# Orders of TensorE and VectorE in the attention of a hybrid decoder layer: left to the scheduler, or written out in the kernel

## The chip, the core and the metric

The kernel runs on one core of a Trainium2 chip. A core has TensorE (PE in the rows; its weight loads are PEld), VectorE (DVE), ScalarE (ACT), GpSimd (POOL), and SyncE (SP), which here only issues DMAs. Each engine takes its instructions in one fixed order and waits at each until what it needs is there. The metric is the device time of one execution in microseconds (us).

## The reference

One decoder layer on 512 tokens of width 1024: RMS norm, one wide input projection, three token mixers (native sparse attention, a gated spatial MLP, an RWKV-7 recurrence), a merge of the three, an output projection, a gated per-layer embedding, a last norm.

```python
def _nsa(q, kc, vc, ks, vs, kw, vw, gate, ...):        # 8 heads of 64, 2 key groups
    ...
    def block(qb):                                     # 128 queries at a time
        p_c = _masked_softmax(q . k_cmp, valid_c)      # 31 compressed keys
        ...
        p_s = _masked_softmax(q . k_sel, valid_s)      # selected blocks: here all 8 of 8
        p_w = _masked_softmax(q . k_win, valid_w)      # window of 512: here all
        return gblk[..., 0:1] * o_c + gblk[..., 1:2] * o_s + gblk[..., 2:3] * o_w

zs = jnp.einsum('bsnc,ncd->bsnd', ys, w_branch[i])     # ys: the three mixers' outputs
merge = jax.nn.sigmoid(mg).reshape(B, S, N_BRANCHES, D)
x = x + jnp.sum(merge * zs, axis=2) @ w_o[i]
```

With 512 tokens the selection takes every block and the window covers every key, so both are plain causal attention with keys of their own.

## The kernel before

Every large product is made of three TensorE matmuls: each float32 operand is split into a high part and a rest (`wh` and `wl` for weights, `hH`/`hL`, `ysH`/`ysL`, `ph`/`pl` for data), and high x high, high x rest, rest x high add up in PSUM. ScalarE makes the high part (a cast), VectorE or GpSimd the rest (a subtraction).

**Attention.** Four query blocks `i` of 128 rows, the last first (`ATT` = 3, 2, 1, 0); block `i` sees `W` = (i+1)*128 keys. In each, two key groups `g`, and in each group two branches `b` (selected, window): 16 steps (i, g, b) with four heads each. A step is made of these parts:
- S0 to S3, the scores of a head: two matmuls of `W` columns and a mask matmul `trib` of 128 columns into `s_ps` (3 buffers); VectorE takes the row maximum `mx`, ScalarE the exponential into `P` with the row sum `sm`.
- norm: VectorE makes 1/`sm` times the branch's gate, and the four heads of `P` are scaled by it. `PS` names the engine for each head: "VVSG" is VectorE, VectorE, ScalarE, GpSimd.
- T0 to Ti, one per 128 keys: four transposes of `P` into `p_ps`; ScalarE casts to `ph`, VectorE subtracts for `pl`.
- O0 to Oi: two matmuls of 512 columns, `pl` then `ph`, into `o_ps` (one buffer). The last one of a group is followed by ScalarE's copy `ot` and two VectorE additions into `nsaY`.

Compressed keys: `sc_c` once per block and a small softmax on VectorE (`pcm`); per group a transpose `pc_ps`, VectorE's `pd`, ScalarE's `ph`, VectorE's `pl`, and the first two products into `o_ps` (`vcst`). `p_ps`, `pc_ps` and `sc_c` share two PSUM buffers (tag "pt").

**Merge.** For each branch b and each of 8 output chunks m, `merge` makes a gate product (24 matmuls of 512 columns from `hH`, `hL`; `sg` is its tanh) and a branch product (12 from `ysH`, `ysL`), multiplies on VectorE and adds on GpSimd into `macc`. Of branch 1, six gates were made earlier and are only loaded. Branches 1 and 2 need nothing from the attention; branch 0 needs all of it. Weights come by DMA into `wr` (4 buffers), ScalarE casts `wh`, GpSimd subtracts `wl` (5 buffers each).

**What sets the order.** The program is handed to a scheduler that runs its own timeline and places every instruction on its engine where it expects it to be ready. `HOLD` holds four chunks of branch 2 behind certain groups of the attention; the rest of the merge of branches 1 and 2 is filled in wherever the scheduler sees TensorE free.

Of the kernel before, what the change touches and what calls it, by code (L numbers as in the profile page):

```python
# [9 lines left out]
F32 = mybir.dt.float32  # L10
# [18 lines left out]
PS = "VVSG"  # L29
ATT = (3, 2, 1, 0)  # L30
HOLD = (-1,) * 12 + (3, 4, 5, 6)
# [14 lines left out]
def hybrid_kernel(ctx, tc, x, p, norm_g, w_in, cmp_w1, cmp_w2, cmp_pe, sg_ln_g, sg_ln_b, sg_w, sg_b,  # L46
# [742 lines left out]
    def merge(b, yH, yL, first, fin, after=()):  # L789
        for m in range(8):  # L790
          with ExitStack() as es:
            if m < len(after) and after[m] is not None:
                es.enter_context(tc.issue_after(after[m]))
            sg = gp.tile([128, 512], F32, tag="sg", name="sg")
            if b == 1 and m < NG:
                SY.dma_start(sg, dr["sg"][m * 128:(m + 1) * 128, :])
            else:
                fm_block(O_MG + b * 1024 + m * 128, 128, lambda ps: S.activation(sg, ps, AF.Tanh, scale=0.5))

            def ev_b(ps):  # L800
                if first:
                    V.scalar_tensor_tensor(macc[:, m, :], sg, 1.0, ps, op0=OP.add, op1=OP.mult)
                else:
                    V.scalar_tensor_tensor(sg, sg, 1.0, ps, op0=OP.add, op1=OP.mult)
                    (V if b == 0 and m == 7 else G).tensor_tensor(macc[:, m, :], macc[:, m, :], sg, OP.add)
                fin(m)
            fm_block(m * 128, 128, ev_b, w_branch[b], yH, yL, 4)
# [5 lines left out]
    anch = []  # L813
    for i in ATT:
        isl = slice(i * 128, (i + 1) * 128)
        W = (i + 1) * 128
        sc = aps.tile([128, 8, 64], F32, tag="pt", name="sc_c", bufs=BP)
        for h in range(8):
            mm(sc[:, h, :], qst[:, h // 2, h % 2, isl], kcst[:, h // 4].rearrange("p a n -> p (a n)"), True, True)
# [10 lines left out]
        gv = gate[:, i, :].rearrange("p (h b) -> p b h", b=3)  # L830
        if i == 0:
            V.scalar_tensor_tensor(sm8, sm8, rowm, gv[:, 0, :], op0=OP.mult, op1=OP.mult)
        else:
            V.tensor_tensor(sm8, sm8, gv[:, 0, :], OP.mult)
        V.tensor_tensor(pcm, pcm, sm8.unsqueeze(2).to_broadcast([128, 8, 32]), OP.mult)
        for g in range(2):
            o_ps = aps.tile([128, 512], F32, tag="o", name="o_ps", bufs=BO)
            pc_ps = aps.tile([128, 128], F32, tag="pt", name="pc_ps", bufs=BP)
            PE.transpose(pc_ps, pcm[:, 4 * g:4 * g + 4, :].rearrange("p h n -> p (h n)"), ident)
            pd = ap_.tile([128, 4, 128], F32, tag="pd", name="pd", bufs=1)  # L840
            ph = ap_.tile([128, 512], R, tag="ph", name="ph", bufs=3)
            pl = ap_.tile([128, 512], R, tag="pl", name="pl", bufs=3)
            V.tensor_tensor(pd, pc_ps.unsqueeze(1).to_broadcast([128, 4, 128]),
                            hm.unsqueeze(2).to_broadcast([128, 4, 128]), OP.mult)
            pd2 = pd.rearrange("p h t -> p (h t)")
            S.copy(ph, pd2)
            V.tensor_tensor(pl, pd2, f(ph), OP.subtract)
            mm(o_ps, vcst[:, g, :], ph, True, False)
            mm(o_ps[0:64], vcst[:, g, 0:64], pl, False, False)
            for b in range(2):  # L850
                P = ap_.tile([128, 4, 512], F32, tag="P", name="P")
                mx = ap_.tile([128, 4], F32, tag="mx", name="mx")
                sm = ap_.tile([128, 4], F32, tag="sm", name="sm")
                for hh in range(4):
                    h = g * 4 + hh
                    s_ps = aps.tile([128, 512], F32, tag="s", name="s_ps", bufs=BS)
                    qs = qst[:, h // 2, h % 2, isl]
                    mm(s_ps[:, :W], qs, kst[b][:, g, 0, :W], True, False)
                    mm(s_ps[:, :W], qs, kst[b][:, g, 1, :W], False, False)
                    mm(s_ps[:, i * 128:W], identb, trib, False, True)  # L860
                    V.tensor_reduce(mx[:, hh:hh + 1], s_ps[:, :W], axis=AX.X, op=OP.max, negate=True)  # L861
                    S.activation(P[:, hh, :W], s_ps[:, :W], AF.Exp, bias=mx[:, hh:hh + 1],  # L862
                                 accum_out=sm[:, hh:hh + 1])
                V.reciprocal(sm, sm)
                V.tensor_tensor(sm, sm, gv[:, 1 + b, g * 4:g * 4 + 4], OP.mult)
                for hh in range(4):
                    if PS[hh] == "S":
                        S.activation(P[:, hh, :W], P[:, hh, :W], AF.Copy, scale=sm[:, hh:hh + 1])
                    else:
                        (G if PS[hh] == "G" else V).tensor_scalar(P[:, hh, :W], P[:, hh, :W], sm[:, hh:hh + 1],  # L870
                                                                  None, op0=OP.mult)
                for kt in range(i + 1):
                    p_ps = aps.tile([128, 512], F32, tag="pt", name="p_ps", bufs=BP)
                    for hh in range(4):
                        PE.transpose(p_ps[:, hh * 128:hh * 128 + 128], P[:, hh, kt * 128:kt * 128 + 128], ident)  # L875
                    ph = ap_.tile([128, 512], R, tag="ph", name="ph", bufs=3)
                    pl = ap_.tile([128, 512], R, tag="pl", name="pl", bufs=3)
                    S.copy(ph, p_ps)  # L878
                    V.tensor_tensor(pl, p_ps, f(ph), OP.subtract)  # L879
                    mm(o_ps[0:64], vst[:, kt, b, g, 0:64], pl, False, False)  # L880
                    last = mm(o_ps, vst[:, kt, b, g, :], ph, False, b == 1 and kt == i)
            anch.append(last)
# [140 lines left out]
```

## Time and profile before

| | |
|---|---|
| runs | 747.08 us median of 3 (744.39 to 748.1) |
| profiled execution | 744.63 us, span 742.8 us |
| TensorE busy in the span | 714.5 us |
| VectorE, ScalarE, GpSimd busy | 408.6, 353.8, 287.0 us |
| first score of the attention, last product into `o_ps` | 378.1 and 562.4 us |
| granted TensorE clock, mean | 0.993 |

The span is the stretch that the profile covers; 1.8 us of the profiled execution lie around it. Positions below are microseconds from the span's start. Matmuls are pipelined: a record of 0.4 us does not mean that the next one starts 0.4 us later, so "busy" overstates how full TensorE is.

### The profile page before, as it was taken

The page shows a single profiled execution, that of the slowest core. Times are in us where ns is not written, and L with a number is a line of the kernel's source. Part 1 is how long each engine was busy: PE and PEld are TensorE (multiplying, and loading weights), DVE is VectorE, ACT ScalarE, POOL GpSimd, SP SyncE. Part 2 cuts the span into 40 slices and gives each one's busy share as a digit, 9 for nine tenths or more (in the row PEclk, how much of TensorE's full clock was granted, in tenths as well). Part 3 has the DMA queues.
Part 4 walks back from the last instruction along what each step waited for, and adds up shares of the span by engine and source line. Part 5 has one row for each costly group of instructions (what it writes and reads, how often), then busy time and mean ns, then how long its engine had stood idle before and what let it go on. Part 6 is the DMA issues. An engine that isn't in the chain of part 4 may idle for free.

```text
span 742.8 us, 13074 instructions
## 1 busy us (share of the span) xinstructions
PE 714.5 (96%) x4941; PEld 606.7 (82%) x4941; DVE 408.6 (55%) x776; ACT 353.8 (48%) x743; POOL 287.0 (39%) x275
## 2 busy tenths in 40 slices
PE   4999999999999999989999999989999999999995
PEld 4888788999878987779877778867877888998995
DVE  6531587758843863565676565397555223226345
ACT  6554555542363342335565554576554333227453
POOL 6444640120220263300144345333445565356563
PEclk9999999999999999999999999999999999999999
DMA  5853122125536364427433212201228334132212
GB/s 194 188 140 100 48 81 71 41 85 146 156 105 224 101 184 117 116 86 232 124 97 103 58 43 71 71 16 42 53 62 268 96 91 127 59 114 72 80 63 114
DMA packets 106689, 78.73 MB, mean 106 GB/s; under 512 B 5569, under 2 KB 97282, under 8 KB 106626
## 3 DMA queue, kind: packets, MB, share of 16 engines
q1 hardware_dynamic: 105890, 75.27, 35.5%
q10 hardware_dynamic: 736, 2.63, 0.9%
q8 instruction: 39, 0.64, 0.4%
q14 instruction: 24, 0.20, 0.1%
HBM read 67.91 MB, written 9.96 MB: 105 GB/s over the span
## 4 chain that ended last, share of the span: by engine, by line
PE 88%; DVE 4%; ACT 2%; DMA 2%; issue 1%; POOL 1%; SPq 1%; ACTq 0%; POOLq 0%; DVEq 0%
PE mm_ps L62 70%; PE s_ps L62 3%; PE o_ps L62 2%; PE g_ps L62 2%; PE p_ps L875 2%; DMA w1t<-in_cmp_w_dram 1%; PE Yp L62 1%; DVE mx L861 1%; PE u_ps L62 1%; ACT wh L78 1%; PE xt_ps L222 1%; PE r_ps L62 1%; PE mx_ps L62 1%; DVE pl L879 1%; PE bk_ps L477 1%
## 5 line engine op out<-in xcount | busy, mean ns | idle before, releaser
L79 POOL TENSOR_TENSOR wl<-wr,wh 128x512 fp32r<-128x512 f32 x144 | 192.6, 1346 | 278.9 <-ACT wh L78 257.6
L78 ACT CAST wh<-wr 128x512 fp32r<-128x512 f32 (+1 forms) x194 | 119.4, 620 | 166.5 <-PE mm_ps L62 114.9
L62 PE MATMUL mm_ps<-hH,wh 128*128 128x512 f32 (+1 forms) x440 | 174.9, 398 | 3.3 <-ACT wh L78 1.9
L62 PE MATMUL mm_ps<-hL,wh 128*128 128x512 f32 (+1 forms) x440 | 171.6, 390 | 0.0
L62 PE MATMUL mm_ps<-hH,wl 128*128 128x512 f32 (+1 forms) x440 | 171.1, 389 | 0.0
L62 PEld LDWEIGHTS mm_ps<-hH,wh 128*128 128x128 f32 x440 | 83.5, 190 | 20.7 <-ACT wh L78 2.2
L62 PEld LDWEIGHTS mm_ps<-hH,wl 128*128 128x128 f32 x440 | 83.2, 189 | 17.4 <-issue 0.2
L62 PEld LDWEIGHTS mm_ps<-hL,wh 128*128 128x128 f32 x440 | 83.6, 190 | 16.5 <-issue 0.2
L62 PE MATMUL mm_ps<-wh,hL 128*128 128x256 f32 (+1 forms) x224 | 65.0, 291 | 0.0
L62 PE MATMUL mm_ps<-wh,hH 128*128 128x256 f32 (+1 forms) x224 | 63.8, 286 | 0.0
L62 PE MATMUL mm_ps<-wl,hH 128*128 128x256 f32 (+1 forms) x224 | 63.7, 285 | 0.0
L79 DVE TENSOR_TENSOR wl<-wr,wh 128x512 fp32r<-128x512 f32 (+1 forms) x50 | 38.0, 768 | 26.8 <-ACT wh L78 26.7
L62 PEld LDWEIGHTS mm_ps<-wh,hL 128*128 128x128 f32 x224 | 42.2, 188 | 1.1 <-issue 0.5
L62 PEld LDWEIGHTS mm_ps<-wh,hH 128*128 128x128 f32 x224 | 42.1, 188 | 1.2 <-issue 0.5
L62 PEld LDWEIGHTS mm_ps<-wl,hH 128*128 128x128 f32 x224 | 42.2, 188 | 0.5
L879 DVE TENSOR_TENSOR pl<-p_ps,ph 128x512 fp32r<-128x512 f32 x40 | 27.1, 685 | 25.7 <-ACT ph L878 25.6
L62 PE MATMUL mm_ps<-ysH,wh 128*128 128x512 f32 x96 | 38.6, 402 | 0.1
L62 PE MATMUL mm_ps<-ysL,wh 128*128 128x512 f32 x96 | 38.4, 400 | 0.2 <-DVE ysL L725 0.2
L62 PE MATMUL mm_ps<-ysH,wl 128*128 128x512 f32 x96 | 38.2, 398 | 0.0
L862 ACT ACTIVATE P<-s_ps,mx 128x512 f32<-128x512 f32 (+3 forms) x64 | 33.4, 531 | 7.9 <-DVE mx L861 5.5
L62 PE MATMUL mm_ps<-wh,mH 128*128 128x256 f32 x128 | 35.9, 286 | 0.0
L62 PE MATMUL mm_ps<-wl,hT 128*128 128x256 f32 x128 | 35.8, 281 | 0.0
(337 smaller groups left out, 1434.6 us busy)
## 6 DMA issues: line engine op xcount, KB each, us to landing
wr<-in_w_in_dram SPq DMA_DIRECT2D x130, 256.0 KB
wr<-in_w_branch_dram SPq DMA_DIRECT2D x24, 256.0 KB
wr<-in_w_o_dram SPq DMA_DIRECT2D x16, 256.0 KB
wr<-in_w_ple_gate_dram SPq DMA_DIRECT2D x16, 256.0 KB
xs__129<-in_x_dram SPq DMA_DIRECT2D x4, 512.0 KB
w1t<-in_cmp_w_dram SPq DMA_DIRECT2D x4, 512.0 KB
x<-in_x_dram ACTq DMA_DIRECT2D x4, 512.0 KB
out_dram<-x SPq DMA_DIRECT2D x8, 256.0 KB
```

Of the source, the lines that this page charges most:

```text
L62: return PE.matmul(o, a, b, start=start, stop=stop, **kw).ins
L78: S.copy(h[:, :m], raw[:, :m])
L79: ph_["l"].tensor_tensor(l[:, :m], raw[:, :m], f(h[:, :m]), OP.subtract)
L222: PE.transpose(ps[:, k, :], xs_[:, t, (4 * a + k) * 128:(4 * a + k + 1) * 128], ident)
L477: PE.transpose(ps[:, c - c0, :], bk[:, c, 0:2].rearrange("p s t -> p (s t)"), ident)
L861: V.tensor_reduce(mx[:, hh:hh + 1], s_ps[:, :W], axis=AX.X, op=OP.max, negate=True)
L862: S.activation(P[:, hh, :W], s_ps[:, :W], AF.Exp, bias=mx[:, hh:hh + 1], accum_out=sm[:, hh:hh + 1])
L875: PE.transpose(p_ps[:, hh * 128:hh * 128 + 128], P[:, hh, kt * 128:kt * 128 + 128], ident)
L879: V.tensor_tensor(pl, p_ps, f(ph), OP.subtract)
```

## The change

The attention and the merge of branches 1 and 2 are written in one interleaved order. TensorE's matmuls and most VectorE instructions there go through `keep_in_program_order` (`pin`), which keeps them in the order in which the code calls them; ScalarE, GpSimd and the DMA queues are still placed by the scheduler.

- `merge_gen` yields before each merge matmul; `deal(n)` issues the next n. There are 432 of them (6 chunks of 12, 10 of 36). `FILL` = (4, 8, 6, 24): 38 around the scores of the first step, then 24 in each of the 16 steps, spread over the step's parts; the last 10 after the attention.
- `ORD` gives the order of the parts within a step. The S parts belong to the next step, L is the previous step's last O, C the two `vcst` products of a group's first step, P the `pc_ps` transpose of the next group in a group's second step. `cmp_` (`sc_c` and its softmax) of the next block comes behind S1 of the step (g, b) = (1, 0).
- `later(n, fn)` runs `fn` at the n-th `tick`; there is a tick behind each part. So `pl` and `nsaY` follow their own part directly on VectorE, and norm and the second half of `cmp_` follow one part later.
- `PS` is "VVSS": ScalarE scales the fourth head, where GpSimd did.
- `HOLD` is gone. `y0`'s four loads of `nz` land in `y0L` itself in place of a `gp` buffer; the merge of branch 0 is as before.

```diff
-PS = "VVSG"
+PS = "VVSS"
 ATT = (3, 2, 1, 0)
-HOLD = (-1,) * 12 + (3, 4, 5, 6)
+FILL = (4, 8, 6, 24)
...
+    def blk_gen(ws, srcH, srcL, nk, evac, ahead):
+        hs, ls = ws
+        ahead()
+        ps = pmm.tile([128, 512], F32, tag="mm", name="mm_ps")
+        for k in range(nk):
+            for j, (w, s) in enumerate(((hs, srcH), (hs, srcL), (ls, srcH))):
+                yield
+                pin(PE.matmul(ps, w[k], s[:, k, :], start=k == 0 and j == 0, stop=k == nk - 1 and j == 2))
+        evac(ps)
...
+    def later(n, fn):
+        late.append([n, fn])
+
+    def tick():
+        for e in list(late):
+            e[0] -= 1
+            if e[0] <= 0:
+                late.remove(e)
+                e[1]()
...
+    def s_(i, g, b, hh):
...
+        mmp(s_ps[:, i * 128:W], identb, trib, False, True)
+        pin(V.tensor_reduce(mx[:, hh:hh + 1], s_ps[:, :W], axis=AX.X, op=OP.max, negate=True))
+        S.activation(P[:, hh, :W], s_ps[:, :W], AF.Exp, bias=mx[:, hh:hh + 1], accum_out=sm[:, hh:hh + 1])
+
+        def norm():
+            pin(V.reciprocal(sm, sm))
+            pin(V.tensor_tensor(sm, sm, gvs[i][:, 1 + b, g * 4:g * 4 + 4], OP.mult))
+            for j in range(4):
+                if PS[j] == "S":
+                    S.activation(P[:, j, :W], P[:, j, :W], AF.Copy, scale=sm[:, j:j + 1])
+                else:
+                    pin(V.tensor_scalar(P[:, j, :W], P[:, j, :W], sm[:, j:j + 1], None, op0=OP.mult))
+        if hh == 3:
+            later(2, norm)
+
+    def t_(i, g, b, kt):
...
+        S.copy(ph, p_ps)
+        later(1, lambda: pin(V.tensor_tensor(pl, p_ps, f(ph), OP.subtract)))
...
+    ORD = {3: "S0 L T0 S1 T1 C S2 O0 S3 T2 O1 T3 P O2", 2: "S0 L T0 S1 T1 C S2 O0 S3 T2 P O1",
+           1: "S0 L T0 S1 C S2 O0 S3 P T1", 0: "S0 L T0 S1 C S2 P S3"}
+    fill = merge_gen(((1, y1H, y1L, True), (2, y2H, y2L, False)))
...
+        for j, act in enumerate(acts):
+            act()
+            tick()
+            deal((j + 1) * FILL[3] // len(acts) - j * FILL[3] // len(acts))
```

TensorE at group (i, g) = (0, 0), up to its two `vcst` products (part C) and the O part behind them. Before:

```order
L62 MATMUL s_ps<-kst_3738,qst 128x128 x2
L62 LDWEIGHTS identb
L62 MATMUL s_ps<-trib,identb 128x128
L62 MATMUL o_ps<-ph,vcst 128x512
L62 MATMUL o_ps<-pl,vcst 64x512
L62 MATMUL o_ps<-pl,vst 64x512
L62 MATMUL o_ps<-ph,vst 128x512
L839 MATMUL pc_ps<-ident,pcm 128x128
```

and in the changed kernel:

```order
L871 MATMUL s_ps<-kst_3738,qst 128x128 x2
L871 LDWEIGHTS identb
L871 MATMUL s_ps<-trib,identb 128x128
L799 MATMUL mm_ps<-hH,wl 128x512
L799 MATMUL mm_ps<-hH,wh 128x512
L799 MATMUL mm_ps<-hL,wh 128x512
L871 MATMUL o_ps<-ph,vcst 128x512
L871 MATMUL o_ps<-pl,vcst 64x512
L799 MATMUL mm_ps<-hH,wl 128x512
L799 MATMUL mm_ps<-hH,wh 128x512
L799 MATMUL mm_ps<-hL,wh 128x512
L799 MATMUL mm_ps<-hH,wl 128x512
```

Where a score, C, an O part and the next `pc_ps` followed each other with no merge product among them, three or four merge products now stand between any two parts of a step of block 0 (two between those of block 3).

VectorE around the norm of a step of block 3: the row maxima, the norm, and the rests `pl` of the transposes. Before:

```order
L879 TENSOR_TENSOR pl<-p_ps,ph 128x512
L865 TENSOR_TENSOR sm<-sm,gate 128x4
L879 TENSOR_TENSOR pl<-p_ps,ph 128x512
L870 TENSOR_SCALAR P<-P,sm 128x512 x2
L802 SCALAR_TENSOR_TENSOR macc<-sg,mm_ps 128x512
```

and in the changed kernel:

```order
L932 TENSOR_REDUCE mx<-s_ps 128x1 x2
L936 RECIPROCAL sm<-sm 128x4
L937 TENSOR_TENSOR sm<-sm,gate 128x4
L942 TENSOR_SCALAR P<-P,sm 128x512 x2
L953 TENSOR_TENSOR pl<-p_ps,ph 128x512 x2
```

The rests of T2 and T3 now stand directly behind the norm of the next step's scores, and so behind the exponential of S3 that the norm waits for.

## Rows read from the trace of the kernel before

**Rows 1.** Page, part 1: busy us, share of the span, instructions of each engine

```profile
PE 714.5 (96%) x4941; PEld 606.7 (82%) x4941; DVE 408.6 (55%) x776; ACT 353.8 (48%) x743; POOL 287.0 (39%) x275
```

**Rows 2.** Windows: stretch, length, then each engine's busy us (instructions), clock, DMA

```profile
380.00:480.00 100.00, 100.00 (x497) 78.34 (x496) 58.88 (x110) 54.34 (x119) 43.60 (x33) 1.00 0.27 72
480.00:520.00 40.00, 36.40 (x211) 27.89 (x210) 33.80 (x83) 26.71 (x73) 13.80 (x12) 1.00 0.12 32
...
540.00:570.00 30.00, 28.09 (x130) 22.00 (x129) 18.25 (x36) 15.68 (x39) 12.15 (x12) 0.94 0.43 132
...
480.00:570.00 90.00, 84.50 (x452) 66.67 (x451) 63.03 (x150) 52.83 (x142) 35.55 (x31) 0.98 0.24 70
```

**Rows 3.** Windows: a stretch of the merge of branch 0, 512-column matmuls alone

```profile
575.00:617.00 42.00, 42.00 (x183) 34.04 (x182) 10.34 (x10) 14.63 (x25) 26.06 (x21) 1.00 0.36 100
```

**Rows 4.** Windows by tile (no POOL column): mm_ps, then o_ps, then s_ps

```profile
480.00:570.00 90.00, 49.72 (x189) 34.95 (x190) 4.11 (x6) 2.96 (x5) 0.98 0.24 70
480.00:570.00 90.00, 18.80 (x53) 7.52 (x52) 4.96 (x12) 3.50 (x6) 0.98 0.24 70
480.00:570.00 90.00, 17.18 (x109) 12.27 (x72) 13.24 (x37) 18.07 (x74) 0.98 0.24 70
```

**Rows 5.** Timeline of TensorE: start, us, what, count, idle before and its releaser

```profile
507.02 0.60 PE L875 MATMUL p_ps<-ident,P 128*128 128x128 f32 x4
...
509.08 0.50 PE L62 MATMUL o_ps<-ph,vcst 128*128 128x512 f32 x1 [0.46 <-ACT ph L846]
510.47 0.45 PE L62 MATMUL o_ps<-pl,vcst 128*64 128x512 f32 x1 [0.90 <-DVE pl L847]
...
513.48 0.23 PE L62 MATMUL s_ps<-trib,identb 128*128 128x128 bf16 x1
...
513.84 0.23 PE L62 MATMUL s_ps<-trib,identb 128*128 128x128 bf16 x1
...
542.00 0.23 PE L62 MATMUL s_ps<-trib,identb 128*128 128x128 bf16 x1
...
542.30 0.23 PE L62 MATMUL s_ps<-trib,identb 128*128 128x128 bf16 x1
...
544.30 0.44 PE L62 MATMUL o_ps<-pl,vcst 128*64 128x512 f32 x1 [1.18 <-DVE pl L847]
```

**Rows 6.** Windows: a stretch of lower granted clock

```profile
545.10:548.50 3.40, 3.40 (x12) 2.84 (x13) 2.83 (x9) 1.19 (x4) 0.89 (x2) 0.50 0.26 80
```

**Rows 7.** Timeline of GpSimd and VectorE at the longest wait

```profile
542.43 1.27 POOL L805 TENSOR_TENSOR macc<-macc,sg 128x512 f32<-128x512 f32 x1 [2.43 <-DVE sg L804]
...
542.78 1.47 DVE L847 TENSOR_TENSOR pl<-pd,ph 128x512 fp32r<-128x512 f32 x1
```

**Rows 8.** Groups by shape, 380 to 570: busy, mean ns, idle before

```profile
L879 DVE TENSOR_TENSOR pl<-p_ps,ph 128x512 fp32r<-128x512 f32 x40 | 27.1, 685 | 25.7 <-ACT ph L878 25.6
L861 DVE TENSOR_REDUCE mx<-s_ps 128x1 f32<-128x512 f32 x16 | 10.8, 682 | 3.3 <-PE s_ps L62 3.2
...
L861 DVE TENSOR_REDUCE mx<-s_ps 128x1 f32<-128x256 f32 x16 | 6.3, 404 | 0.4 <-PE s_ps L62 0.4
...
L862 ACT ACTIVATION_READ_ACCUMULATOR P<-s_ps,mx 128x1 f32 x64 | 13.0, 204 | 0.0
L862 ACT ACTIVATE P<-s_ps,mx 128x512 f32<-128x512 f32 x16 | 10.9, 690 | 3.9 <-DVE mx L861 3.7
...
L862 ACT ACTIVATE P<-s_ps,mx 128x256 f32<-128x256 f32 x16 | 7.5, 477 | 0.7 <-DVE mx L861 0.6
...
L870 POOL TENSOR_SCALAR P<-P,sm 128x512 f32<-128x512 f32 x4 | 7.0, 1744 | 5.3 <-DVE sm L865 2.8 <-PE s_ps L62 2.2 <-PE pc_ps L839 0.2
```

**Rows 9.** Timeline: TensorE's mask product, then VectorE's maximum, norm and scaling

```profile
412.92 0.23 PE L62 MATMUL s_ps<-trib,identb 128*128 128x128 bf16 x1
...
413.19 0.69 DVE L861 TENSOR_REDUCE mx<-s_ps 128x1 f32<-128x512 f32 x1 [1.31 <-PE s_ps L62]
...
415.59 0.17 DVE L864 RECIPROCAL sm<-sm 128x4 f32<-128x4 f32 x1
...
415.99 1.32 DVE L870 TENSOR_SCALAR P<-P,sm 128x512 f32<-128x512 f32 x2
```

More of the change, by code (lines that the diff above doesn't have):

```diff
@@ L787, in hybrid_kernel @@
     macc = gp.tile([128, 8, 512], F32, name="macc", bufs=1)
[L789 to L794, printed above, removed]
+    pin = tc.keep_in_program_order
+    def blk_gen(ws, srcH, srcL, nk, evac, ahead):
[7 more added lines that the diff above has]
+        evac(ps)
@@ new lines, in merge_gen, with ask @@
+    def merge_gen(jobs):
+        todo = []
+        for b, yH, yL, first in jobs:
+            for m in range(8):
+                if not (b == 1 and m < NG):
+                    todo.append((b, m, "g", yH, yL, first))
+                todo.append((b, m, "o", yH, yL, first))
+        got = {}
+        def ask(n):
+            if n < len(todo) and n not in got:
+                b, m, kind, *_ = todo[n]
+                got[n] = (wparts([(w_in, O_MG + b * 1024 + m * 128, 128)], 8) if kind == "g"
+                          else wparts([(w_branch[b], m * 128, 128)], 4))
+        ask(0)
+        sg = None
+        for n, (b, m, kind, yH, yL, first) in enumerate(todo):
+            if kind == "g" or (b == 1 and m < NG):
+                sg = gp.tile([128, 512], F32, tag="sg", name="sg")
+            if kind == "g":
+                yield from blk_gen(got.pop(n), hH, hL, 8,
+                                   lambda ps, sg=sg: S.activation(sg, ps, AF.Tanh, scale=0.5), lambda: ask(n + 1))
+                continue
@@ new lines, in merge_gen, with merge @@
+            yield from blk_gen(got.pop(n), yH, yL, 4, ev_b, lambda: ask(n + 1))
+    def merge(b, yH, yL, first, fin):
+        for m in range(8):
+            sg = gp.tile([128, 512], F32, tag="sg", name="sg")
+            fm_block(O_MG + b * 1024 + m * 128, 128, lambda ps: S.activation(sg, ps, AF.Tanh, scale=0.5))
+            def ev_b(ps):
+                V.scalar_tensor_tensor(sg, sg, 1.0, ps, op0=OP.add, op1=OP.mult)
+                (V if m == 7 else G).tensor_tensor(macc[:, m, :], macc[:, m, :], sg, OP.add)
@@ L830, in hybrid_kernel @@
[L830 to L882, printed above, removed]
@@ new lines, in hybrid_kernel, with deal @@
+    ORD = {3: "S0 L T0 S1 T1 C S2 O0 S3 T2 O1 T3 P O2", 2: "S0 L T0 S1 T1 C S2 O0 S3 T2 P O1",
+           1: "S0 L T0 S1 C S2 O0 S3 P T1", 0: "S0 L T0 S1 C S2 P S3"}
+    fill = merge_gen(((1, y1H, y1L, True), (2, y2H, y2L, False)))
+    def deal(n):
+        for _ in range(n):
+            next(fill, None)
+    steps = [(i, g, b) for i in ATT for g in range(2) for b in range(2)]
+    cmp_(3)
+    tick()
+    for hh in range(4):
+        s_(*steps[0], hh)
+        tick()
+        deal(FILL[0])
@@ L890, in hybrid_kernel @@
+    o_(*prev, prev[0])
+    tick()
+    tick()
+    for _ in fill:
+        pass
     at_ctx.close()
     nsa_ctx.close()
-    hold = [None if h < 0 else anch[h] for h in HOLD]
-    merge(1, y1H, y1L, True, lambda m: None, hold[:8])
-    merge(2, y2H, y2L, False, lambda m: None, hold[8:])
     y0H, y0L = ytiles()
-    for q in range(4):
-        zs = gp.tile([128, 512], F32, tag="sg", name="zs")
-        SY.dma_start(zs, dr["nz"][q * 128:(q + 1) * 128, :])
-        V.tensor_tensor(nsaY[:, q, :], nsaY[:, q, :], zs, OP.mult)
-        split(y0H[:, q, :], y0L[:, q, :], nsaY[:, q, :], 0.5)
@@ L908, in hybrid_kernel @@
     fg = ep.tile([128, 1024], F32, name="fg")
+    for q in range(4):
+        zs = f(y0L[:, q, :])
+        SY.dma_start(zs, dr["nz"][q * 128:(q + 1) * 128, :])
+        V.tensor_tensor(nsaY[:, q, :], nsaY[:, q, :], zs, OP.mult)
+        split(y0H[:, q, :], y0L[:, q, :], nsaY[:, q, :], 0.5)
     for t in range(4):
```

122 lines of the change are left out of this document (101 added, 21 removed).

## The prediction

> **What bounds the kernel now.** I read the page first: TensorE is busy 96% of the span [rows 1], and nothing else comes near. So a change of order can only win what TensorE loses inside the attention. The windows say where that is: from 380 to 480 TensorE never stands idle, from 480 to 520 it shows 3.6 us idle in 40, and from 540 to 570 1.9 us in 30 [rows 2]. In the first stretch VectorE has 58.9 us of work in 100, in the second 33.8 in 40 [rows 2]. The scheduler used up its merge products early; what was left of the attention then came faster than VectorE and ScalarE could follow.
>
> Idle time understates the loss, because a record outlasts the matmul's turn. The turn is read where nothing waits: 183 records in 42 us [rows 3], one of them reaching over an edge, so 0.231 us for a matmul of 512 columns. Now I count the work between 480 and 570. 452 records [rows 2]: 189 of the merge and 53 of `o_ps` [rows 4], all of 512 columns, are 242 x 0.231 = 55.9 us. 109 records are scores [rows 4], which is 37 heads (109 / 3, rounded up); a head takes 0.30 us at 128 columns (mask product to mask product, 542.00 to 542.30) and 0.36 at 256 (513.48 to 513.84) [rows 5]. The sixteen of block 0 and the other 21 are 4.8 + 7.6 = 12.4 us; four of those 21 are wider still, which I leave out. The remaining 101 records are transposes and `sc_c`, 0.11 us each (four of them last 0.60 us with the tail of 0.27 of the last: 0.33 / 3) [rows 5], 11.1 us. Together 79.4 us in 90: about **10.2 us** are lost, taking 0.4 off for the wide heads.
>
> What are they? Waits of a `vcst` product for the rest `pl` or the high part `ph` of the compressed keys (0.46, 0.90 and 1.18 us of idle in the three rows shown) [rows 5], smaller ones like them, and 3.4 us at half the clock, 1.2 instead of 2.4 GHz, from 545.1, right behind the longest wait [rows 6]; at half speed that costs 1.7 us.
>
> **The change, part by part.**
>
> *Merge products dealt out.* The number of matmuls stays as it was. Each step gets 24 merge products, 24 x 0.231 = 5.5 us, where some had none. C now stands at least three parts behind P, each part with its products: 2 us and more, for a chain of `pd`, `ph` and `pl` of about 0.7 us each (the row of `pl` has 685 ns [rows 8]). All of the C waits go, and with them the half clock behind one. The end is covered too: the last 10 products and the first gate of branch 0 (24) stand between the last O and what needs `nsaY`, 34 x 0.231 = 7.9 us, where now idle time shows up to 570. If nothing new waits, the gain is the 10.2 us. Loads of weights: 12 products use one load and GpSimd's `wl` takes no more than before, so I put no cost there.
>
> *The norm one part later, on a fixed order.* This is what can wait anew. VectorE must do norm of the next step's scores, then `pl` of T2. From the mask product of S3 at 0: maximum starts at 0.27 (412.92 to 413.19) [rows 9] and takes 0.68, exponential 0.69, read of the sum 0.20 [rows 8], reciprocal and gate 0.40 (415.59 to 415.99) [rows 9], two scalings, then `pl` 0.69. Without the scalings 2.9 us. The two scalings take 1.32 us [rows 9], but GpSimd was scaling its head beside them, 1.74 us long [rows 8]; a lower end is what the same two would take at 0.45 each, an estimate from the shorter of them being started at 0.40 behind the other. So `pl` of T2 is ready at 3.8 to 4.2.
>
> TensorE gets there earlier. In **block 3** it passes eight merge products (1.85), T2 and T3 (0.44 each), O1 (0.46) and the tail of S3 (0.1): 3.3 us to O2, which needs that `pl`; in a group's second step P stands there instead and needs the PSUM buffer that the same `pl` reads. Wait 0.5 to 0.9. The pipelining of the records (next instruction starts before the last one's end) takes some 0.2 off; I take 0.45, for the three steps whose next has 512 columns: 1.4 us.
>
> In **block 2** the way to the product is nine merge products, T2, O1, S0: 3.6 us, and the chain is shorter by the narrower maximum and exponential: no wait, 0.2 us in sum for chance. In **block 1** T1 is followed only by S0 and then L, which needs T1's rest: eight products (1.85), T1 0.44, S0 0.36, tail 0.1: 2.75. Chain: 0.27 + 0.40 + 0.48 + 0.20 [rows 8] + 0.40, scalings 0.6 (half the columns), `pl` 0.69: 3.0. Wait 0.25, and where P stands in the step, `pd` and its `pl` lie in VectorE's order as well (2 x 0.6) against two products and a transpose more (0.6): 0.8. Two of each: 2.1 us. In **block 0** T0 comes two parts behind S3 and waits for the scaled `P`: about 0.3 us in four steps, by ScalarE's two scalings, and in the last two steps VectorE also has `nsaY` times `nz` and its split in between: 1.3 us in all, the term I know least.
>
> *ScalarE instead of GpSimd for the fourth head.* 16 scalings more on ScalarE (about 0.7 us each at 512 columns, like its exponential [rows 8]). It had 54.3 us in 100 and 26.7 in 40 [rows 2]; a step of block 3 now brings it about 9.3 us in 11.5. It stays under TensorE, so nothing by itself; queueing there is in the terms above.
>
> *What VectorE meets on GpSimd.* `pl` from `pd` took 1.47 us beside GpSimd's `macc` addition, the `pl` of the same size from PSUM 0.685 [rows 7, 8]. By these rows alone only an operation that reads two SBUF tensors is hurt, and a scaling stays at the 1.32 for two: block 3's wait would be 0.9, 1.3 us more than my sum. The Trainium skill, SBUF — State Buffer, section "Who interferes with whom", says that a GpSimd operation and a VectorE one in a two-port mode, scalings named among them, also hold each other up wholly, whoever came first; by that, taking the scaling off GpSimd shortens the pair, and the sum would be as I made it. The pair's 1.32 us, where the second record is the long one, agrees with that but does not prove it.
>
> *`HOLD`, the loads of `nz`, the table of early parts*: the loads come earlier than before and nothing waits for them; nothing before the attention moves on any engine that sets the time.
>
> **Sum.** Lost before 10.2; new waits 1.4 + 0.2 + 2.1 + 1.3 = 5.0 (3 where nothing meets GpSimd or queues on ScalarE, 9 where every step loses 0.55). Gain 5.2 us on the profiled execution's 744.63: 739.4. That execution lies 2.45 under the median of the runs, so on the scale of the median **741.9**.
>
> **The rivals.**
> 1. *Nearly all is kept* (new waits under 2 us). For it: the loss was in C waits, and these go by a wide margin. Against it: the arithmetic of blocks 3 and 1 above. 747.1 - 9 = 738.
> 2. *Given back.* The norm chain is later than I made it, because VectorE is not free when S3 ends (block 3: maxima 2.7, `pl` 2.7, merge 1.3, the rest 2.5, about 9.3 of 11.5 us per step) or because ScalarE stands at a weight cast that waits for a buffer, with exponentials queued behind it. New waits of 8 to 12: 745 to 749, no change to be told. For it: 25.6 us of VectorE's idle time was for `ph` [rows 8], so it does stand behind ScalarE.
> 3. *Slower.* The same chain, with a price in all 16 steps: O, L or T0 waits for the norm. At 10.2 / 16 = 0.64 us per step the change wins nothing; from 0.87 it is slower by over 0.5%; at 1.0 us 747.1 + 5.8 = 753. For it: the chain of 3.8 to 4.2 against 3.3 shows the margin is gone in the blocks with most work. Against it: block 2 has room, and a late TensorE gives VectorE time to catch up.
> 4. *The clock.* The half clock came behind a wait of 1.18 us, after others [rows 5, 6], while 480 to 520 with 3.6 us idle kept the full clock [rows 2]. If the new short waits made such a stretch in every block, 4 x 1.7 = 6.8 us go back: 749. The Trainium skill, TensorE: Matmul & The Clock Gate, section "A second HAM failure mode: psum-queue depth-cycling", tells of a kernel whose frequent tiny idle times made the clock swing; here 480 to 520 speaks against it.
>
> **How the numbers follow.** Chances: the forecast (new waits 3 to 7, 739.9 to 744) 0.42; rival 1 0.20; rival 2 0.26; rival 3 0.08; rival 4 0.04. Measurement tells about 0.5% from no change, 3.7 us: faster means under 743.4, slower over 750.8. The forecast lies under 743.4 for most of its part (0.35), with rival 1 that is 0.55 faster; 0.09 slower (rival 3 and the top of 4); 0.36 the same. The likeliest case's own range is 739 to 744; that of all, down to the full gain of 10.2 and up through rival 2, is 736.5 to 749.5, and leaves out the far half of rivals 3 and 4.
>
> **What would show it.** In the new profile, no `vcst` product waits over 0.3 us and no stretch of lower clock lies between 380 and 570. TensorE's idle time before transposes or `o_ps` is spread over the steps, at O2 and P of block 3, L of block 1, T0 of block 0, with VectorE `pl` or ScalarE `P` as the releaser; the count of 79.4 us holds, and the attention's end comes about 5 us earlier. I am wrong if the waits sit at the merge products (weights late), if VectorE's idle time in the attention goes up instead of TensorE's going down, or if a step of block 3 takes over 12.1 us (11.5 and a wait of 0.6).

## The result: slower by 1%

The changed kernel takes 753.8 us, median of 4 runs (753.56 to 754.08), beside 746.13 for the kernel before (4 runs, 744.39 to 748.1). The ratio is 1.0103, with a 95% interval of 1.0088 to 1.0119. The forecast was 741.9, with a range up to 749.5.

The page's first part, in the columns of [rows 1]:

```profile
PE 719.1 (96%) x4941; PEld 608.1 (81%) x4941; DVE 414.3 (55%) x776; ACT 363.6 (48%) x759; POOL 268.7 (36%) x259
```

The numbers of matmuls and of VectorE instructions are those of before; 16 scalings moved from GpSimd to ScalarE. The span is 751.9 instead of 742.8 us, so TensorE waits more. The waits of TensorE from 375 to 575, grouped by line and releaser; first the kernel before:

```profile
PE o_ps L62 <- DVE pl L847: 2.1, 2, 1.2
PE o_ps L62 <- DVE nsaY L888: 0.8, 1, 0.8
PE o_ps L62 <- DVE pl L879: 0.7, 2, 0.4
PE o_ps L62 <- ACT ph L846: 0.5, 1, 0.5
PE p_ps L875 <- DVE P L870: 0.4, 1, 0.4
PE s_ps L62 <- ACT P L862: 0.3, 1, 0.3
PE mm_ps L62 <- DVE ysL L725: 0.2, 1, 0.2
```

and the changed kernel:

```profile
PE o_ps L871 <- DVE pl L953: 7.7, 5, 3.3
PE mm_ps L799 <- DVE macc L831: 1.7, 1, 1.7
PE s_ps L871 <- ACT P L933: 0.3, 1, 0.3
PE pc_ps L905 <- DVE pl L953: 0.3, 1, 0.3
```

The waits for the compressed keys (`pl` L847, `ph` L846) are gone, as forecast. In their place stand five waits of an O part for the rest `pl` of a transpose (L953), and one of a merge product at the start for VectorE's `macc`. The sum went from 5.0 to 10.0 us.

Where they stand is told by windows (busy time of PE, PEld, DVE, ACT, POOL, then the granted clock, as in [rows 2]):

```profile
380.00:392.00 12.00, 10.04 (x47) 6.99 (x46) 10.19 (x19) 6.73 (x16) 3.65 (x3) 1.00 0.26 69
392.00:430.00 38.00, 37.45 (x196) 27.57 (x195) 28.00 (x52) 24.97 (x52) 8.03 (x7) 1.00 0.28 76
430.00:434.00 4.00, 2.48 (x13) 1.58 (x12) 3.45 (x8) 2.38 (x5) 0.93 (x1) 1.00 0.02 4
...
478.00:485.00 7.00, 4.78 (x20) 4.00 (x21) 3.54 (x8) 2.71 (x6) 0.76 (x1) 0.76 0.16 40
...
519.00:529.00 10.00, 6.71 (x31) 5.32 (x30) 5.02 (x12) 3.97 (x11) 1.49 (x2) 0.83 0.11 27
529.00:570.00 41.00, 41.00 (x209) 32.61 (x208) 25.63 (x56) 24.60 (x66) 16.92 (x14) 1.00 0.26 70
```

Not a loss in every step: four places. Between them TensorE is as good as full; the stretches left out, 434 to 478 and 485 to 519, show 43.85 us busy of 44 and 33.68 of 34. The first is the attention's start. The other three are one step in each of blocks 3, 2 and 1, and the same step each time: group 1, branch 0, where part S1 is followed by `cmp_`, the compressed scores and softmax of the next block. Two of these places also show a lower clock (0.76 and 0.83 in their windows), as the kernel before does in [rows 6]; and so does a stretch at 320, ahead of everything that the change touches:

```profile
320.00:327.00 7.00, 6.48 (x71) 5.65 (x72) 4.45 (x10) 1.46 (x4) 0.00 (x0) 0.52 0.17 59
```

The two inside the attention cost 7 x 0.24 + 10 x 0.17 = 3.4 us, against the 1.7 of before. At 320 the same instructions in the same order ran 2.1 us faster in the profile of before: they start at 319.95 there and at 319.99 here, and the third 512-column product behind them at 324.70 and 326.87.

The account of the 9.1 us between the two profiles goes by the windows from the attention's first score to TensorE's last matmul, in the kernel before, in the changed kernel and in the later version e10:

```profile
378.08:735.35 357.27, 351.28 (x2058) 296.28 (x2056) 181.65 (x364) 177.41 (x403) 172.67 (x146) 1.00 0.28 83
380.34:744.03 363.69, 353.20 (x2058) 295.36 (x2057) 186.65 (x363) 186.15 (x418) 154.02 (x130) 0.99 0.27 81
382.26:735.98 353.72, 350.00 (x2058) 292.98 (x2057) 180.74 (x363) 186.26 (x418) 154.03 (x130) 1.00 0.29 84
```

The window is 6.4 us longer than before: 4.5 of idle time (10.5 for 6.0) and 1.7 of half clock (3.4 for 1.7), with 0.2 left. It begins 2.3 later, 2.1 of that from the stretch at 320; and 0.4 more lies behind the last matmul, which I do not trace. TensorE's busy time less what the half clock costs is 349.6, 349.8 and 350.0 in the three rows: the idle time and the clock account for the differences.

Now the longest wait, back to its origin. TensorE at O1 of step (1, 1, 0), with start, us, operation, and the idle time ahead with its releaser:

```profile
516.31 0.23 PE L871 MATMUL s_ps<-trib,identb 128*128 128x128 bf16 x1
...
524.24 0.45 PE L871 MATMUL o_ps<-pl,vst 128*64 128x512 f32 x1 [3.29 <-DVE pl L953]
```

and VectorE ahead of that `pl`:

```profile
514.55 0.42 DVE L880 TENSOR_TENSOR pcm<-sc_c,cmask 128x256 f32<-128x256 f32 x1 [0.19 <-PE sc_c L871]
...
515.93 1.25 DVE L885 TENSOR_TENSOR pcm<-pcm,mx 128x256 f32<-128x256 f32 x1
517.11 0.68 DVE L833 SCALAR_TENSOR_TENSOR sg<-sg,mm_ps 128x512 f32<-128x512 f32 x1
...
518.38 0.79 DVE L894 SCALAR_TENSOR_TENSOR sm<-sm,rowm,gate 128x8 f32<-128x8 f32 x1
519.21 0.42 DVE L897 TENSOR_TENSOR pcm<-pcm,sm 128x256 f32<-128x256 f32 x1
519.55 0.75 DVE L932 TENSOR_REDUCE mx<-s_ps 128x1 f32<-128x256 f32 x2
521.54 0.18 DVE L936 RECIPROCAL sm<-sm 128x4 f32<-128x4 f32 x1 [1.25 <-ACT P L933]
521.75 0.17 DVE L937 TENSOR_TENSOR sm<-sm,gate 128x4 f32<-128x4 f32 x1
521.96 1.63 DVE L942 TENSOR_SCALAR P<-P,sm 128x256 f32<-128x256 f32 x2
523.51 0.68 DVE L953 TENSOR_TENSOR pl<-p_ps,ph 128x512 fp32r<-128x512 f32 x1
```

S2's scores are there at 516.5. Their maximum is taken at 519.55, 3 us late, because eight operations of the compressed softmax (four of them left out here) and a merge operation hold VectorE from 514.55 on in the written order. So ScalarE's exponentials are late, the norm waits 1.25 us for them, and `pl` of T1, whose transposes were done by 519.5, stands behind the norm (ScalarE's cast `ph`, which it also needs, ran from 520.47 to 521.05, itself behind S2's exponential). VectorE is busy 55% of the span, as before. It is late because of what its written order puts ahead.

Part of this wait is not the order. GpSimd makes a `wl` beside two of these operations, the one at 515.93 and the pair of scalings at 521.96. In the run e3 below, where no GpSimd operation meets them, the same two of the same step take 0.43 and 0.61 us instead of 1.25 and 1.63, 1.8 us less in the chain:

```profile
515.61 1.29 POOL L79 TENSOR_TENSOR wl<-wr,wh 128x512 fp32r<-128x512 f32 x1 [3.36 <-ACT wh L78]
```

```profile
522.12 0.43 DVE L886 TENSOR_TENSOR pcm<-pcm,mx 128x256 f32<-128x256 f32 x1
...
526.82 0.61 DVE L943 TENSOR_SCALAR P<-P,sm 128x256 f32<-128x256 f32 x2
```

No run takes GpSimd's share out by itself.

### The profile page after: what moved, and what is told of

It is laid out like the page before. It is cut to its first block, busy times and chain, and to the rows that moved or that the text cites. A ratio compares the mean times of both kernels' runs of the same rounds, so it can differ in the third digit from the quotient of the medians.

```text
span 751.9 us, 13019 instructions
## 1 busy us (share of the span) xinstructions
PE 719.1 (96%) x4941; PEld 608.1 (81%) x4941; DVE 414.3 (55%) x776; ACT 363.6 (48%) x759; POOL 268.7 (36%) x259
## 4 chain that ended last, share of the span: by engine, by line
PE 85%; DVE 7%; ACT 3%; issue 2%; DMA 1%; POOL 1%; SPq 1%; POOLq 0%; ACTq 0%; DVEq 0%
PE mm_ps L62 56%; PE mm_ps L799 11%; PE o_ps L871 3%; PE s_ps L871 3%; PE p_ps L950 2%; PE g_ps L62 2%; DMA w1t<-in_cmp_w_dram 1%; PE Yp L62 1%; DVE P L942 1%; PE u_ps L62 1%; PE r_ps L62 1%; DVE pl L953 1%; DVE mx L932 1%; ACT P L933 1%; PE mx_ps L62 1%
## 5 line engine op out<-in xcount | busy, mean ns | idle before, releaser
L62 PE MATMUL mm_ps<-hH,wh 128*128 128x512 f32 (+1 forms) x360 | 142.2, 395 | 2.9 <-ACT wh L78 1.7
L62 PE MATMUL mm_ps<-hL,wh 128*128 128x512 f32 (+1 forms) x360 | 139.6, 388 | 0.0
L62 PE MATMUL mm_ps<-hH,wl 128*128 128x512 f32 (+1 forms) x360 | 139.4, 388 | 0.0
L62 PEld LDWEIGHTS mm_ps<-hH,wh 128*128 128x128 f32 x360 | 68.6, 191 | 17.3 <-ACT wh L78 1.9
L62 PEld LDWEIGHTS mm_ps<-hH,wl 128*128 128x128 f32 x360 | 68.3, 190 | 14.8 <-DVE wl L79 0.3
L62 PEld LDWEIGHTS mm_ps<-hL,wh 128*128 128x128 f32 x360 | 68.5, 190 | 13.7 <-issue 0.2
L932 DVE TENSOR_REDUCE mx<-s_ps 128x1 f32<-128x512 f32 (+3 forms) x64 | 30.6, 485 | 16.5 <-PE s_ps L871 16.2
L953 DVE TENSOR_TENSOR pl<-p_ps,ph 128x512 fp32r<-128x512 f32 x40 | 27.5, 688 | 21.7 <-ACT ph L952 21.6
L62 PE MATMUL mm_ps<-wh,lT 128*128 128x256 f32 x128 | 35.8, 281 | 0.0
L62 PE MATMUL mm_ps<-wh,hT 128*128 128x256 f32 x128 | 35.8, 285 | 0.0
```

The lines of the kernel that those rows point to most:

```text
L62: return PE.matmul(o, a, b, start=start, stop=stop, **kw).ins
L932: pin(V.tensor_reduce(mx[:, hh:hh + 1], s_ps[:, :W], axis=AX.X, op=OP.max, negate=True))
L953: later(1, lambda: pin(V.tensor_tensor(pl, p_ps, f(ph), OP.subtract)))
```

## The experiments

Theory A: the compressed softmax in one piece makes VectorE about 3 us late in three steps (and at the start), and the norm ahead of `pl` hands that on to TensorE. Theory B: ScalarE has one scaling too many. Theory C: the norm's new place is too late by itself, in every step. Edits are against the changed kernel.

**e1, the softmax spread.** It begins two steps earlier, and its operations are dealt out over 21 parts. In the first softmax, at the attention's start, the sum stands one part earlier.

```diff
-            if w == "S1" and (g, b) == (1, 0) and i > 0:
+            if w == "S1" and (g, b) == (0, 1) and i > 0:
...
+        a = (0, 0, 0, 2, 2, 2) if i == 3 else (2, 5, 12, 15, 18, 21)
+        later(a[0], lambda: pin(V.tensor_reduce(mx8, pcm, axis=AX.X, op=OP.max)))
+        later(a[1], shift)
```

> Theory A (compressed softmax): in the changed kernel the eight VectorE operations of the next block's compressed softmax stand together in one step of each block, ahead of the maxima of S2 and S3, and push norm and `pl` back; that made the waits of 1.5, 2.4 and 3.3 us at O2, O2 and O1 and the two stretches of half clock behind them (about 1.4 us each). Here the same operations begin two steps earlier and stand two to seven parts apart. By A these three waits fall under 0.5 us each and the time falls by 8 to 10 us, to 744 to 746. Theory B (ScalarE has one scaling too many) and theory C (the norm one part later is too late in every step): nothing they blame is touched, 752 to 755, with the three waits in place.

Measured: 746.7 us (12 runs), 7.1 less; ratio to the kernel before 1.0002 (0.9989 to 1.0014). The waits of TensorE (the profile is of the quickest of the twelve, 744.3 us, and shows no half clock in the attention):

```profile
PE s_ps L871 <- ACT P L937: 2.6, 1, 2.6
PE o_ps L871 <- DVE pl L957: 1.4, 3, 0.8
PE pc_ps L909 <- DVE pl L957: 0.5, 1, 0.5
```

The three waits of 1.5 to 3.3 us are gone, with the same work on VectorE. What is left is the start (2.6, now before S3, where it was 1.7 before a merge product) and short ones in blocks 3 and 1. B and C are wrong as whole causes: nothing that they blame was touched. The gain is a little under A's 8 to 10.

**e2, the softmax ahead.** All four before the attention's first score, for the scheduler to place (`for i in ATT: cmp_(i)`, without `pin`).

> All four compressed softmaxes ahead of the attention's written order and not pinned, so that the scheduler puts them into the projections. Theory A: the three waits go as with the spread version, and VectorE has 3.4 us less to do in three steps of the attention: 743 to 747. If the work at the attention's start (VectorE is late with the rests of the keys there, 2.5 us lost) grows instead by some of it, up to 749. Theories B and C: 752 to 755.

Measured: 751.6 us (6 runs). A miss, nearer to B's and C's 752 than to A's 749. But the three waits that B and C keep are gone here too; the scheduler put all four softmaxes where the attention begins, S3 of the first step waits 5.8 us, and 5 us and more at half clock follow. The window there, and the wait:

```profile
384.00:397.00 13.00, 6.43 (x37) 4.83 (x37) 12.88 (x39) 5.43 (x12) 1.30 (x1) 0.93 0.15 40
```

```profile
PE s_ps L871 <- ACT P L931: 5.8, 1, 5.8
```

VectorE is full there (12.88 of 13 us), with the rests of the keys in among the softmaxes. Work taken from three places landed on a fourth that was already late.

**e3, the softmax longer.** The maximum over the compressed scores is taken five times.

```diff
-        pin(V.tensor_reduce(mx8, pcm, axis=AX.X, op=OP.max))
+        for _ in range(5):
+            pin(V.tensor_reduce(mx8, pcm, axis=AX.X, op=OP.max))
```

> The maximum over the compressed scores is taken five times instead of once (the same result each time), 4 x 0.42 = 1.7 us more on VectorE at each of the four places. Theory A: this lands in full on the three waits, 5 us, and in part on the attention's start, 1 to 2: 758.5 to 761. Theories B and C: the work is hidden under VectorE's idle time, 753 to 755.

Measured: 758.05 us (4 runs), 4.3 more, just under A's range. Hidden it is not, so B and C fail again. But it did not land where A put it. The waits for `pl` went only from 7.7 in 5 to 8.3 in 7, where A had 5 us more; the longest even fell, from 3.3 to 2.8; GpSimd did not meet its chain here. Most came at the start, whose wait went from 1.7 to 3.6 with half clock behind it; half clock follows three waits instead of two.

**e4, the fourth head off ScalarE.** `PS = "VVSG"`.

> Only the engine of the fourth head's scaling is put back, to GpSimd, as in the kernel before. Theory A: the three waits stay, 753 to 756 (GpSimd's scaling takes 1.74 us against 0.7, so T0 may wait a little longer). Theory B: ScalarE is relieved of 0.5 to 0.7 us per step, the waits of 1.5 to 3.3 us fall by half or more, and the time goes to 749 or less.

Measured: 758.1 us (4 runs), 4.3 more, above both ranges. But the changed code knows only "S" and, for any other letter, VectorE; so the head went to VectorE, not GpSimd (its scalings of 512 columns, by shape: 12 in place of 8). ScalarE was relieved all the same, and the waits for `pl` grew from 7.7 to 10.1 us. Theory B says that they shrink. What weighs more is VectorE's chain: 0.48 us more in it at 512 columns, and the three long waits grow to 2.3, 2.7 and 3.5. As a test of B it is not clean, since VectorE got what ScalarE lost.

**e13, the fourth head on GpSimd itself.** As in the kernel before (`G.tensor_scalar` for "G").

> The changed kernel with the fourth head's scaling on GpSimd itself, as in the kernel before (the earlier run with this name in its label had put it on VectorE, third in the pair's row, since the changed code knows only ScalarE and VectorE). Theory A: the three waits stay; the pair of VectorE's scalings, 0.88 us for 512 columns beside ScalarE in the changed kernel, goes back to 1.32 beside GpSimd, 0.3 to 0.5 us later for `pl` in the steps that wait, and the three long waits and the two or three short ones grow by that each: 755 to 757.5. Theory B (ScalarE's added scaling delays the exponentials): the three waits shrink by 0.5 us or more each, 752 or less. If GpSimd's 1.74 us is hidden and the pair is not hurt: 753 to 754.5.

Measured: 755.96 us (4 runs), 2.2 more, in A's range. Two of the three long waits grew, to 2.4 and 2.8, and so did the short ones; the third fell from 3.3 to 2.6, which A did not have: its pair of scalings met GpSimd's short scaling here (0.83 us), not the `wl` (1.63). B's shrinking by 0.5 us each did not come. By shape, the scalings of the changed kernel and of this one:

```profile
L942 DVE TENSOR_SCALAR P<-P,sm 128x512 f32<-128x512 f32 x8 | 3.5, 485 | 0.1
```

```profile
L944 DVE TENSOR_SCALAR P<-P,sm 128x512 f32<-128x512 f32 x8 | 5.3, 702 | 0.1
...
L942 POOL TENSOR_SCALAR P<-P,sm 128x512 f32<-128x512 f32 x4 | 7.1, 1771 | 8.5 <-DVE sm L937 6.1 <-ACT ph L954 2.4
```

So within the changed kernel the move from GpSimd to ScalarE gains 2.2 us: two scalings of 512 columns on VectorE take 0.43 us less without GpSimd's beside them.

**e7, the norm's place alone.** The norm one part later still in blocks 3 to 1, behind the rest of the step's last T or last but one, and T1 ahead of P in block 1. The softmax stays in one piece.

```diff
-            later(2, norm)
+            later(nn, norm)
...
-                acts.append(lambda w=w: s_(*nx, int(w[1])))
+                acts.append(lambda w=w: s_(*nx, int(w[1]), 3 if i > 0 else 2))
...
-           1: "S0 L T0 S1 C S2 O0 S3 P T1"
+           1: "S0 L T0 S1 C S2 O0 S3 T1 P"
```

> The changed kernel with that place of the norm alone; the compressed softmax stays in one piece. Theory A says the softmax makes VectorE late by some 3 us in those steps, and the norm's place only hands this on to `pl`: O1 or O2 no longer waits, T0 (two parts, about 2 us, further on) waits for the rest: the three waits of 7.2 us in sum fall to 1 to 4, and of the two stretches of half clock one or both go: 747 to 751. Theory C (the norm's place is the whole cause): as good as the spread version, 746.7 or less. If the place does not matter at all: 753 to 755.

Measured: 747.7 us (12 runs), 6.1 less, in A's range and 1 us short of C's, with no stretch of half clock between 380 and 570. The waits in the three dear steps fall from 7.2 to 2.3 us in sum, and T0 waits anew in two other steps of block 1 (1.2 and 0.4). The long wait of block 1 became two short ones, one for `pl` and one, a part later, for the scaled `P`:

```profile
519.97 0.45 PE L871 MATMUL o_ps<-pl,vst 128*64 128x512 f32 x1 [0.87 <-DVE pl L953]
...
521.84 0.72 PE L950 MATMUL p_ps<-ident,P 128*128 128x128 f32 x4 [0.49 <-DVE P L942]
```

As A has it: VectorE still has the softmax in one piece, and the order decides whether TensorE has to know. And C as first put fails outright: a norm still later was better.

**e12, both.** e1 and e7 together.

> Spread and the later norm together, with 24 products per step as in the changed kernel. The place of the norm alone was worth 6.1 us (753.8 to 747.7), the spread alone 7.1 (to 746.7). If the two are links of one chain (the softmax makes VectorE late, the norm ahead of `pl` hands it on), they do not add up: 744.5 to 746.5. If they were two causes apart, their gains would add up: 740 to 742.

Measured: 747.6 us (12 runs), no faster than either alone. They do not add up: two links of one chain, of which either one broken is enough. It is above the range given. In its profile T0 waits for the scaled `P` in four places, 2.0 us in sum, where e1 had no such wait, and the start's wait of 2.6 us has a stretch of half clock behind it.

**e5, e6, e9, the dealing.** e5 is e1 with `FILL = (8, 8, 6, 23)`; e6 is e5 with the norm of e7; e9 is e1 with eight products more at the start (`FILL = (6, 8, 6, 24)`) and 22 per step in block 2.

> The spread version with FILL = (8, 8, 6, 23): 16 merge products more around the scores of the first step, one fewer in each of the 16 steps. Theory A with its second part (at the start VectorE has the keys' rests, the compressed softmax and the first maxima in one fixed order, and TensorE gets to S3 2.6 us too soon): 16 x 0.231 = 3.7 us more of products there cover the wait, and the steps have 0.23 us less each, of which the waits of block 3 and 1 take some 1 us: 744 to 745.5. Rival (the start is held by something that moves with it, such as a weight that arrives late): 746 to 748, with a wait left before P.

> As the last one, and the norm one part later still (behind the rest `pl` of the step's last T or last but one) in blocks 3, 2 and 1, with T1 ahead of P in block 1. If the small waits left at O2, P and O1 (0.05 to 0.81 us, 2 us in sum in the spread version) come from the norm standing ahead of `pl` on VectorE, they go: 742 to 744. If the norm is now late for T0 of the next step, the waits move there: 745 to 747.

> The spread version with eight merge products more at the start, taken from the four steps of block 2 (22 instead of 24), which showed no wait even with 23. If the loss of the version with 23 everywhere came from steps that have no product to spare in blocks 3, 1 and 0, then here the start's wait of 2.6 us shrinks by up to 1.8 and nothing new waits: 744.5 to 746. Rival: block 2 has no slack either once it gives two, its waits come back at its O2 and T0, 746.5 to 748.

Measured: 748.0 (8 runs), 747.5 and 747.8 us (12 each). Three misses of theory A in one direction. In e5 the start's wait fell from 2.6 to 1.0, but one product less, 0.23 us, in each step made the waits in the steps grow from 1.9 to 6.7 us:

```profile
PE o_ps L871 <- DVE pl L957: 4.6, 6, 1.6
PE pc_ps L909 <- DVE pl L957: 1.3, 1, 1.3
PE mm_ps L799 <- DVE kst L763: 1.0, 1, 1.0
PE p_ps L954 <- DVE P L946: 0.8, 1, 0.8
```

These waits stand in blocks 3, 1 and 0. There a step's chain through VectorE and ScalarE is as long as what TensorE has to do in it, and products lent to another place are missing. In e6 the waits went from `pl` to T0 (2.5 us in five), as its second reading had it. Block 2, which showed no wait over 0.2 us with 23, had two with 22, of 0.23 and 0.94 us (e9), as the rival said; the others of e9 stand at the start and in blocks 3 and 1.

**e10 and e11, the best version.** e10 is e9 with the later norm in block 3 alone; in e11 GpSimd also makes the compressed keys' `pl`.

```diff
-                acts.append(lambda w=w: s_(*nx, int(w[1])))
+                acts.append(lambda w=w: s_(*nx, int(w[1]), 3 if i == 3 else 2))
...
-        later(1, lambda: pin(V.tensor_tensor(pl, pd2, f(ph), OP.subtract)))
+        G.tensor_tensor(pl, pd2, f(ph), OP.subtract)
```

> As the last one, with the norm behind the rest of T2 in the steps of block 3 alone, where O2 and P wait 0.27 to 0.50 us in the spread version (1.05 us in sum). If these come from the norm ahead of `pl`: 1 us faster than the last one. If VectorE's work in those steps as a whole is late, the waits move to T0 and nothing is won.

> As the last one, with the rest `pl` of the compressed keys (two SBUF operands, 0.96 and 1.15 us on VectorE beside GpSimd's work in two places of the changed kernel, 0.69 without) made by GpSimd in each of the eight steps with a P. If VectorE's total in those steps sets the waits left: 0.5 to 1.5 us faster than the last one. If GpSimd (1.3 us each) then holds VectorE's other operations on two SBUF operands, or C waits for it: the same or 1 to 2 us slower.

Measured: 744.8 and 744.4 us (12 runs each), beside 746.2 for the kernel before (35 runs); ratios 0.9973 (0.9961 to 0.9985) and 0.9972 (0.9959 to 0.9984). Both beat both kernels, the one before by 0.3%. The waits of e10:

```profile
PE o_ps L871 <- DVE pl L957: 2.0, 3, 0.9
PE s_ps L871 <- ACT P L937: 0.5, 1, 0.5
PE mm_ps L799 <- DVE kst L763: 0.4, 1, 0.4
```

Where the steps are long (block 3), `pl` ahead of the norm takes away every wait at O2 and P; where they are short it does not pay, since T0 comes too soon (e6, e7, e12). The step from e9 to e10 is 3.0 us, where 1 was expected; in the two profiles 2.3 of it are waits (5.2 and 2.9), all at O2 and P of block 3, for which the expectation took the 1.05 of the spread version. From e10 to e11 nothing can be told apart, so neither reading of e11 is shown.

**e8, the kernel before once more.**

> The kernel before once more, for its profile. The changed kernel and the four experiments show half the clock near 320 us, ahead of every changed instruction, behind the wait of 1.9 us that the kernel before has too; its profile does not show it. If that is chance, a profile of the kernel before at about 747 us shows the stretch (2.2 us) and one at about 745 does not. If it belongs to the change, no profile of the kernel before shows it.

Measured: 746.76 us, and this profile has the stretch:

```profile
320.00:327.00 7.00, 5.27 (x69) 4.72 (x70) 5.11 (x12) 1.14 (x3) 0.00 (x0) 0.64 0.25 76
```

So the stretch is not the change's: the kernel before has it too. Of the 15 profiles 13 show the stretch, the first one of before and that of e11 do not. This second profile also lacks the stretch of [rows 6], and has one of 3.4 us at 216 that the first does not have; five of the experiments' profiles have that one too.

## Why the prediction was wrong

**What bounds it, and what was lost.** Right in kind, too large in size. The waits for the compressed keys went, the half clock behind the longest of them too, and the attention's end is covered; with the order mended (e10) the waits from 375 to 575 are 2.9 us instead of 5.0. But the gain was set at the 10.2 us of the count. Of these TensorE showed 5.5 as idle time and 1.7 as half clock, 7.2 together. The other 3.0 came back in no version: busy time less half clock stays at 349.3 to 350.0 us in the kernel before, the changed one, e1, e10 and e11, though e10 and e11 have only 3.7 and 4.5 us of idle time in the whole window. So the prediction's first term, "the gain is the 10.2 us", could not be had in full, even with no new wait.

**The failed step: "The norm one part later, on a fixed order".** The prediction counted VectorE's chain from the mask product of S3, as if VectorE were free then: maximum, exponential, norm, `pl`. In a usual step it was nearly so. The waits that this sum foresaw are 0.3 at O2, 0.3 at P and 0.25 at L (7.7 less the three long ones, and the wait of `pc_ps`), 0.8 us where it had 5.0. But in three of the 16 steps the eight operations of `cmp_` stand ahead of S2's and S3's maxima. The sum gave them no price at all, although the change had moved them into that order; in the rows they hold VectorE from 514.55 to 519.6, in part because of GpSimd. They cost 7.2 us of waits (1.5, 2.4 and 3.3), and 3.4 us of half clock came behind two of these. e1 (taken out of these steps: 7.1 us back) and e7 (the norm behind `pl`: 6.1 back) show it, and e12 that these are one chain. e4 (another 0.48 us in the same chain: 4.3 more) agrees; e3 shows that the softmax's length costs time, but mostly at the start.

On the scale of the profiled executions the forecast was 739.4, and 753.6 came. Of the 14.2 between, 5.0 are waits (10.0 instead of 5.0), 3.4 half clock that the forecast had at nothing, 3.0 the loss that could not be won back, and 2.1 the stretch at 320, which is bad luck and not the change; 0.7 is left. That the waits of the usual steps were put 4 us too high hid part of the missing term.

**The start** was overlooked too. The rests of the keys, the first compressed softmax and the first maxima were put into one order on VectorE, and a merge product there waits 1.7 us for `macc`, which stands behind three maxima. The kernel before had VectorE just as full from 380 to 392, and TensorE without a wait:

```profile
380.00:392.00 12.00, 12.00 (x55) 8.85 (x54) 11.85 (x25) 8.18 (x19) 4.40 (x4) 1.00 0.34 91
```

There the scheduler had put each `macc` in between the maxima, so that the products could go on. That this is the difference is read from the two orders; no run moves `macc` alone.

**ScalarE for GpSimd.** "Nothing by itself" holds for ScalarE as far as the runs tell (e4 and e13 relieved it and lost time). For VectorE it was too little: 2.2 us were won, by e13. The rows of before gave two readings of the pair's 1.32 us. The runs settle it. In the changed kernel the pair takes 0.88 us at 512 columns where GpSimd is idle, and 1.63 at only 256 columns where GpSimd's `wl`, 1.34 us long, starts beside it:

```profile
430.49 0.88 DVE L942 TENSOR_SCALAR P<-P,sm 128x512 f32<-128x512 f32 x2
...
522.09 1.34 POOL L79 TENSOR_TENSOR wl<-wr,wh 128x512 fp32r<-128x512 f32 x1 [2.95 <-ACT wh L78]
```

So a scaling, with one SBUF tensor as its operand, is held too, against the reading "by these rows alone" in the prediction. The Trainium skill, SBUF — State Buffer, section "Who interferes with whom", has the shared port pair as an exclusive lock for a whole instruction. The pair beside `wl` agrees: it ends at 523.59, 0.16 us behind the `wl`. Beside GpSimd's own scaling, in e13, the pair is held for less than that:

```profile
432.12 1.32 DVE L944 TENSOR_SCALAR P<-P,sm 128x512 f32<-128x512 f32 x2
432.29 1.75 POOL L942 TENSOR_SCALAR P<-P,sm 128x512 f32<-128x512 f32 x1 [4.34 <-DVE sm L937]
```

It takes 0.44 us more than without GpSimd and ends 0.6 us ahead of GpSimd's scaling, so there the measurement goes against a lock for the whole instruction.

**The rivals.** Rival 2, at 0.26, named the condition (VectorE is not free when S3 ends) and the size of the waits, 8 to 12 us where 10.0 came; its time, 745 to 749, was too low because it set them against the 10.2 and had no half clock. Rival 3 had the mechanism (the norm chain late for O and L) and nearly the time, 753, but asked for a price in all 16 steps, 16 us, and got a chance of 0.08 for that. Three dear steps were enough; that 16 less 10.2 came near the measured loss is luck. Rival 4's stretches came behind two of the four long waits.

**The range** ended at 749.5 because every unknown in it was a variation of the usual step. The step that differs from the others was not looked at, and nor was the 10.2 itself.

## What to carry to other kernels

Where an order is written out for an engine that was scheduled, list everything that the engine does in each kind of step, the rare ones first: an insertion of 4 to 5 us once in each of three blocks, on an engine that is 55% busy, cost more than all usual steps together. Spread such work over many slots, and put the operation that the bound engine needs next ahead of the one that waits for a third engine. Filler is a budget: look for where the chain per step is as long as the filler, because there no product can be lent. And a loss that is counted from prices per matmul should be held against idle time and clock before it is booked as a gain.

## What the runs showed of the hardware

TensorE's clock falls to its lower level behind some waits and not behind others like them. The same 1.88 us wait at 320, in the same instructions, was followed by it in 13 profiles of 15, at a price of 2.1 us. The wait of 1.18 us of [rows 5] was followed by it in the first profile of the kernel before; the second has the same wait, of 1.18 us at 547.88, and the full clock behind it (1.00 from 548 to 552). In the changed kernel the waits of 2.4 and 3.3 us were, those of 1.5 and 1.7 were not. The runs of the kernel before beside the experiments spread with it, though not by it alone: those at a mean clock of 0.993 or 0.994 took 744.9 to 746.2 us, those at 0.989 took 745.7 to 747.9, those at 0.991 took 745.1 to 748.2.
